# Streamed projections whose left operands start at the right operands' byte offset within 512

## The chip, the cores and the metric

The kernel runs on one core of a Trainium2 chip. The metric is the device time of one execution in microseconds; lower is better. Engines are named as the profile names them: PE (matrix multiply) and PEld (its load of left operands), DVE (vector), ACT (scalar), POOL (GpSimd), SP (sync, which here only issues DMAs).

## The reference

One decoder layer on a sequence of 1024 tokens, model width 1024, all in float32:

```python
h = rmsnorm(x, g_mix)
z = h @ w_in                                   # 1024 x 7168
rnn_x, rnn_y, conv_b, conv_c, conv_x, gate_rnn, gate_conv = split(z)
rnn_x = causal_depthwise_conv(rnn_x, conv4_w) + conv4_b
y_rnn = gelu(rnn_y) * rg_lru(rnn_x, ...)       # gates: block diagonal products, then a scan over tokens
y_conv = conv_b * causal_depthwise_conv(conv_c * conv_x, conv3_w)
merged = sigmoid(gate_rnn) * y_rnn + sigmoid(gate_conv) * y_conv
x = x + merged @ w_out
g, u = split(rmsnorm(x, g_ffn) @ w_gate_up)    # 1024 x 5632
x = x + (silu(g) * u) @ w_down
x = x + sigmoid(rmsnorm(x, g_ple) @ w_ple_gate) * (p @ w_ple)
return rmsnorm(x, g_final)
```

## The kernel before

Every float32 product is done in three passes over exact halves of its operands: `split` rounds an operand to a high half (ACT, a copy into float32r) and subtracts it for the low half (DVE), and `mm` (lines 108 to 112) issues low times high, high times low and high times high. A matmul of PE takes a left operand of 128x128, which PEld loads, and streams a right operand of 128x512 past it. The big products use Strassen's scheme in Winograd's form: seven block products in place of eight.

There are five stages. The head computes `p @ w_ple` and the first norm. The **input projection** (line 728) and **gate/up** (line 797) are the two streamed projections: `stream` (line 207) keeps the seven right operands, made of the activations, in tiles of the pool `ops`, and streams the weights through as left operands. For each product it loads a quarter of 128x512 (`part`), adds quarters where the scheme wants it, and makes the left operand `wop` of it, in `high` (line 248, ACT) and `low` (line 253, DVE). A product is 12 matmuls. The input projection has 28 pairs of channel blocks, so 28 x 7 x 12 = 2352 matmuls, and the recurrence that runs between them adds 192 (`rg`); gate/up has 22 pairs, 1848 matmuls. Between and behind these stages the **output projection** and **down** (`outer`, line 336) make both operands in `ops`, and the per-layer gate (line 860) ends the program.

A scheduler sets the order on each engine from the order of the code and from priorities; `stream` makes an operand two products ahead of its use. The only DMAs that POOL issues are some loads of the output projection and of down (`load` with `nc.gpsimd`, lines 746, 819 and 822); all others are SP's.

Where a tile lies follows from the pools. At the bottom of each partition of SBUF lie 16,384 bytes of scratch for the DMA descriptors that POOL makes, then constants, then `ops` (seven tiles of 16,384 bytes), the small tiles `sm`, and above them the pools of the stage: `w1`, `w2`, `ws`, `wp`, `ev`, `e0`, `wq` (line 205). The left operands lie in `wp` and `wq`; the last two of every seven products use `wq`. Before the change the starts are these, as remainders modulo 512 bytes (all the pieces of an operand that a matmul reads lie a multiple of 512 bytes from its start):

| operand | pool | remainder |
|---|---|---|
| right operands of both streamed projections; both operands of `outer` | `ops` | 128 |
| left operands `wop`, both streamed projections | `wp` | 320 |
| both operands of the recurrence's products, `xo` and `rg_w` | `wp` | 320 |
| left operands `wop`, input projection | `wq` | 448 |
| left operands `wop`, gate/up | `wq` | 320 |

`wq` differs between the stages since the four tiles of `e0` below it are 516 floats in the input projection (2064 bytes, padded to 2080) and 512 floats in gate/up.

## Time and profile before

| | us |
|---|---|
| median of three runs | 1460.82 |
| the three runs | 1458.82 to 1462.44 |
| span of the profiled execution, first to last instruction | 1458.2 |
| its own time outside the span | not listed; the runs lie 0.6 to 4.2 above the span |
| PE busy | 1437.6 (99%) |
| DVE, ACT busy | 1077.8 (74%), 781.7 (54%) |
| input projection on PE | 44.4 to 633.8 |
| output projection and norm on PE | 633.8 to 716.1 |
| gate/up on PE | 716.1 to 1143.8 |
| down, gate, last norm | 1143.8 to 1458.2 |

The busy time of a matmul in the profile includes its run through the array, which overlaps with the next matmul's (393 ns each, though they start some 230 ns apart). So the pace of PE is read from start to start: in the timeline, where consecutive matmuls with the same operands' names are merged to one row, the start of a row less the start of the row before, divided by the count.

### The profile page before, as it was taken

What the parts mean: (1) busy time and instruction counts of PE and PEld (TensorE: products, weight loads), DVE (VectorE), ACT (ScalarE), POOL (GpSimd) and SP (SyncE); (2) the same over time, 40 slices, a digit from 0 to 9 for tenths busy, and PEclk for the clock granted to TensorE, in tenths of its full rate; (3) what the DMA queues carried; (4) which work ended last, traced back from release to release, by engine and by line L of the source; (5) the groups of instructions that cost most, each with busy time, mean ns of one, the idle gap of its engine ahead of it and who ended that gap; (6) DMA issues with size and microseconds to landing.
All of it is one profiled execution on the core that took longest, in us unless ns stands there. A gap on an engine that the chain in (4) does not pass through costs nothing.

```text
span 1458.2 us, 17521 instructions
## 1 busy us (share of the span) xinstructions
PE 1437.6 (99%) x6348; PEld 1176.0 (81%) x6348; DVE 1077.8 (74%) x1617; ACT 781.7 (54%) x1214; POOL 10.6 (1%) x20
## 2 busy tenths in 40 slices
PE   8999999999999999999999999999999999999997
PEld 6787888888888888878888888888888888888886
DVE  6989757965697669689796555555554899995854
ACT  7757746754775467545773333333333343346764
POOL 0000000000000000000000000000000000000000
PEclk9999999999999999999999999999999999999999
DMA  8321221122112211381522222222223761524431
GB/s 317 111 87 51 75 77 52 52 79 74 53 55 75 77 51 59 111 286 53 172 81 101 87 82 85 87 88 83 76 80 106 255 231 37 195 87 141 148 145 58
DMA packets 76742, 153.77 MB, mean 105 GB/s; under 512 B 7920, under 2 KB 7920, under 8 KB 76656
## 3 DMA queue, kind: packets, MB, share of 16 engines
q1 hardware_dynamic: 74768, 145.84, 29.9%
q0 software_dynamic: 1888, 6.82, 1.4%
q8 instruction: 50, 0.82, 0.2%
q14 instruction: 36, 0.29, 0.1%
HBM read 120.12 MB, written 32.51 MB: 105 GB/s over the span
## 4 chain that ended last, share of the span: by engine, by line
PE 90%; DVE 3%; DMA 3%; ACT 2%; issue 1%; SPq 0%; DVEq 0%; ACTq 0%
PE X L111 46%; PE Y L111 23%; PE Z L111 11%; PE pg L874 6%; PE rg L111 3%; PE tp L151 1%; DMA pe_d<-peo 1%; DMA xt<-x_d 1%; DMA xt<-in_x 0%; ACT b L85 0%; DVE a11b L100 0%; DMA act_d<-a 0%; DMA a<-m_d 0%; DMA m_d<-v 0%; DVE v L722 0%
## 5 line engine op out<-in xcount | busy, mean ns | idle before, releaser
L111 PE MATMUL X<-t,wop 128*128 128x512 f32 x1800 | 431.3, 393 | 0.0
L111 PEld LDWEIGHTS X<-t,wop 128*128 128x128 f32 x1800 | 338.2, 188 | 76.6 <-DVE wop L254 0.3
L250 ACT CAST wop<-part 128x512 fp32r<-128x512 f32 x300 | 183.7, 621 | 213.8 <-PE X L111 67.4
L254 DVE TENSOR_TENSOR wop<-part,wop 128x512 fp32r<-128x512 f32 x300 | 204.8, 689 | 89.0 <-ACT wop L250 87.8
L111 PE MATMUL Z<-b,wop 128*128 128x512 f32 x600 | 146.7, 393 | 0.4 <-ACT r_late L192 0.4
L111 PE MATMUL X<-b,wop 128*128 128x512 f32 x600 | 147.0, 393 | 0.0
L111 PE MATMUL Y<-b,wop 128*128 128x512 f32 x600 | 146.4, 393 | 0.0
L111 PE MATMUL Y<-t,wop 128*128 128x512 f32 x600 | 146.2, 393 | 0.0
L111 PEld LDWEIGHTS Z<-b,wop 128*128 128x128 f32 x600 | 112.5, 188 | 26.8 <-ACT r_late L192 0.9
L111 PEld LDWEIGHTS Y<-b,wop 128*128 128x128 f32 x600 | 112.8, 188 | 25.5
L111 PEld LDWEIGHTS Y<-t,wop 128*128 128x128 f32 x600 | 112.8, 188 | 25.2
L111 PEld LDWEIGHTS X<-b,wop 128*128 128x128 f32 x600 | 112.6, 188 | 24.6
L874 PE MATMUL pg<-b,a 128*128 128x512 f32 (+1 forms) x408 | 88.4, 378 | 0.0
L111 PE MATMUL X<-t,s 128*128 128x512 f32 x360 | 85.8, 392 | 0.0
L874 PEld LDWEIGHTS pg<-b,a 128*128 128x128 f32 x408 | 73.4, 188 | 14.6
L254 DVE TENSOR_TENSOR wop<-s,wop 128x512 fp32r<-128x512 f32 x50 | 34.5, 689 | 59.5 <-ACT wop L250 59.5
L111 PEld LDWEIGHTS X<-t,s 128*128 128x128 f32 x360 | 66.8, 188 | 13.9 <-DVE t L86 0.5
L271 ACT COPY p<-Y 128x512 f32<-128x512 f32 x50 | 29.2, 583 | 72.6 <-PE Y L111 72.6
L271 ACT COPY s<-X 128x512 f32<-128x512 f32 x50 | 29.2, 588 | 59.2 <-PE X L111 58.9
L271 ACT COPY u<-X 128x512 f32<-128x512 f32 x50 | 29.2, 584 | 49.6 <-PE X L111 49.1
L435 DVE TENSOR_TENSOR xt<-X,xt 128x512 f32<-128x512 f32 x64 | 43.8, 686 | 14.5 <-PE X L111 13.6
L111 PE MATMUL rg<-xo,rg_w 128*128 128x512 f32 x192 | 47.1, 393 | 0.1
(172 smaller groups left out, 1939.7 us busy)
## 6 DMA issues: line engine op xcount, KB each, us to landing
part<-in_w_in SPq DMA_DIRECT2D x120, 256.0 KB, 2.6
part<-in_w_gu SPq DMA_DIRECT2D x96, 256.0 KB, 2.7
act_d<-a SPq DMA_DIRECT2D x44, 256.0 KB, 2.4
x_d<-xt SPq DMA_DIRECT2D x32, 256.0 KB, 2.0
bc<-in_w_down SPq DMA_DIRECT2D x10, 512.0 KB, 5.8
a<-act_d SPq DMA_DIRECT2D x10, 512.0 KB, 5.9
xt<-in_x SPq DMA_DIRECT2D x8, 512.0 KB, 8.0
pe_d<-peo SPq DMA_DIRECT2D x16, 256.0 KB, 2.9
```

What stands on the lines that cost most here:

```text
L111: nc.tensor.matmul(ps, lhs(i), rhs(j), start=start and first and n == 0, stop=last and n == 2, skip_group_check=not start)
L151: nc.tensor.transpose(ps[:, b * P:(b + 1) * P], xt[b][:, kk * P:(kk + 1) * P], ident)
L250: nc.scalar.copy(t[:, 0], s)
L254: sub(t[:, 1], s, t[:, 0].bitcast(F32))
L271: nc.scalar.copy(t, ps)
L435: add(piece, ps, piece)
L874: nc.tensor.matmul(ps, left[k // 4](i, k % 4)[:, c:c + P], right[k // 4, dh][:, j, k % 4, r], start=n + k == 0, stop=n == 2 and k == 7)
```

## The change

Three edits of sizes; no instruction is added or taken away, and on every engine the instructions stand in the same order with the same waits. The DMA scratch is halved to 8,192 bytes, which moves all tiles down by 8,192 and makes room. A filler of 320 bytes, `line`, lies between `sm` and the pools of the stages. The tiles that the input projection takes from `e0` get 544 floats (2,176 bytes, four are 8,704 = 17 x 512), of which 516 are used. With that `ops`, `wp`, `wq` of both stages, and `w1`, `w2`, `ws` and `ev` all start at remainder 128. The rest of the difference takes comments and docstrings out.

```diff
     sm = ctx.enter_context(tc.tile_pool(name="sm", bufs=2))
+
+    ctx.enter_context(tc.tile_pool(name="line", bufs=1)).tile([P, 80], F32, name="line")
     pp = ctx.enter_context(tc.tile_pool(name="pp", bufs=8, space=bass.MemoryType.PSUM))
...
         def ztile(name, early=False):
-            return (sp["e0"] if early else zp).tile([P, H + 4], F32, tag="z", name=name)
+
+            return (sp["e0"].tile([P, 544], F32, tag="z", name=name)[:, 0:H + 4] if early
+                    else zp.tile([P, H + 4], F32, tag="z", name=name))
...
-    nc = bacc.Bacc("TRN2", target_bir_lowering=False, num_devices=1)
+    nc = bacc.Bacc("TRN2", target_bir_lowering=False, num_devices=1, dynamic_dma_scratch_size=8192)
```

| operand | before | after |
|---|---|---|
| `ops` | 128 | 128 |
| `wp` (`wop`, `xo`, `rg_w`) | 320 | 128 |
| `wq`, input projection | 448 | 128 |
| `wq`, gate/up | 320 | 128 |

## Rows read from the trace of the kernel before

**Rows 1.** Page, part 1: busy us (share of the span) and instructions.

```profile
span 1458.2 us, 17521 instructions
PE 1437.6 (99%) x6348; PEld 1176.0 (81%) x6348; DVE 1077.8 (74%) x1617; ACT 781.7 (54%) x1214; POOL 10.6 (1%) x20
```

**Rows 2.** Stretches: length, busy us (instructions) of each engine, PE clock, DMA.

```profile
44.40:633.80 589.40, 589.25 (x2547) 478.15 (x2546) 453.04 (x724) 366.54 (x565) 1.56 (x2) 1.00 0.23 74
716.10:1143.80 427.70, 427.23 (x1881) 350.10 (x1880) 265.58 (x385) 172.37 (x288) 2.54 (x4) 1.00 0.28 91
```

**Rows 3.** Timeline, PE, input projection: start, us, engine, line, operands, count.

```profile
314.36 2.95 PE L111 MATMUL X<-t,wop 128*128 128x512 f32 x12
317.15 2.96 PE L111 MATMUL Z<-b,wop 128*128 128x512 f32 x12
319.95 2.92 PE L111 MATMUL Y<-b,wop 128*128 128x512 f32 x12
322.71 5.66 PE L111 MATMUL X<-t,wop 128*128 128x512 f32 x24
328.20 2.91 PE L111 MATMUL Y<-t,wop 128*128 128x512 f32 x12
...
333.70 2.96 PE L111 MATMUL X<-t,wop 128*128 128x512 f32 x12
336.50 2.96 PE L111 MATMUL Z<-b,wop 128*128 128x512 f32 x12
339.30 2.96 PE L111 MATMUL Y<-b,wop 128*128 128x512 f32 x12
342.10 5.76 PE L111 MATMUL X<-t,wop 128*128 128x512 f32 x24
347.70 2.96 PE L111 MATMUL Y<-t,wop 128*128 128x512 f32 x12
```

**Rows 4.** Timeline, PE, gate/up.

```profile
819.70 5.66 PE L111 MATMUL X<-t,wop 128*128 128x512 f32 x24
825.20 2.91 PE L111 MATMUL Y<-t,wop 128*128 128x512 f32 x12
```

**Rows 5.** Timeline, PE, output projection and down: both operands in `ops`.

```profile
658.02 11.04 PE L111 MATMUL Y<-t,s 128*128 128x512 f32 x48
668.90 11.09 PE L111 MATMUL X<-t,s 128*128 128x512 f32 x48
679.83 11.04 PE L111 MATMUL Y<-b,s 128*128 128x512 f32 x48
...
1151.97 8.32 PE L111 MATMUL Z<-b,a 128*128 128x512 f32 x36
1160.13 8.32 PE L111 MATMUL Y<-t,s 128*128 128x512 f32 x36
```

**Rows 6.** Timeline, PE, two products of the recurrence between products of the stream.

```profile
231.02 2.89 PE L111 MATMUL rg<-xo,rg_w 128*128 128x512 f32 x12
233.75 2.93 PE L111 MATMUL Y<-b,wop 128*128 128x512 f32 x12
236.51 2.93 PE L111 MATMUL rg<-xo,rg_w 128*128 128x512 f32 x12
239.28 2.93 PE L111 MATMUL X<-t,wop 128*128 128x512 f32 x12
```

**Rows 7.** Chain that ended last, around 102 to 135: start, us, what.

```profile
102.80 0.59 ACT z L512
...
134.63 0.71 DVE xo L578
135.38 2.59 PE rg L111 x10
```

**Rows 8.** The same chain at the ends of the two streamed stages.

```profile
622.86 2.76 PE Y L111 x12
...
1132.98 2.76 PE Y L111 x12
```

**Rows 9.** POOL's timeline: its DMA issues, and what it waited for.

```profile
625.92 1.56 POOL L392 DMA_DIRECT2D b<-in_w_out  x2 [624.61 <-DMA bc<-in_w_out]
1138.78 1.28 POOL L392 DMA_DIRECT2D b<-in_w_down  x2 [511.31 <-DVE b L86]
```

**Rows 10.** DMA view: POOL's issues, KB each, median us from issue to landing.

```profile
b<-in_w_down POOLq DMA_DIRECT2D x5, 512.0 KB, 5.1
a<-act_d POOLq DMA_DIRECT2D x5, 512.0 KB, 6.2
```

## The prediction

> **What bounds the kernel now.** The page's first part comes first: PE is busy 99% of the span, DVE 74%, ACT 54% [rows 1]. That alone doesn't say that PE is limited by its own pace, since a busy matmul may be a slow one. [...]

> Then the timeline, read from start to start. Where both operands lie in `ops`, at the same remainder of 128, 48 matmuls take 668.90 - 658.02 = 10.88 us, and 36 take 1160.13 - 1151.97 = 8.16 us [rows 5]: **226.7 ns** each, in two stages and with very different neighbours. In gate/up, with the left operand at 320, 24 matmuls take 825.20 - 819.70 = 5.50 us, **229** ns each [rows 4]. In the input projection the products that use `wq` (remainder 448) take 317.15 - 314.36 = 2.79 and 336.50 - 333.70 = 2.80 us for 12, **233** ns each; those behind them that use `wp` (320) run now at 5.49 / 24 = 229 ns (322.71 to 328.20), now at 5.60 / 24 = 233 ns (342.10 to 347.70) [rows 3]. All of these are matmuls of the same shape at the same clock with no wait between them. The pace differs by where the left operand lies, and `wp` products in the input projection take over the pace of one of two patterns, depending on what ran before them. The same `wp` products in gate/up, where no product lies at 448, stay at 229.

> The recurrence's products are the near miss that tells most. Both of their operands lie at 320: the same remainder, but not 128. One of them takes 233.75 - 231.02 = 2.73 us for 12 [rows 6], 227.5 ns: near the pace of `outer`, with the excess over 226.7 only 0.1 us per product, though it comes from a product at another remainder and is followed by one. So what counts is the difference of the two starts, not that the left one is at 128.

> **The change part by part.** *Offsets.* Order, waits, sizes and data are as before; so the work on PE is the same matmuls at another pace. Price per matmul after: 226.7 ns by the rows of `outer` [rows 5] at the best, 227.5 by the recurrence's row [rows 6] at the worst of the rows with equal remainders that I take as the nearest; I use 226.8, since the rows of `outer` have both operands at 128, which is what all will have. The slower pieces that the rows of `outer` also hold (679.83 - 668.90 = 10.93 us for 48, 227.7 ns) are one in several.

> Input projection: 589.25 us over 28 x 7 x 12 + 192 = 2544 matmuls is 231.6 ns, and without the few tenths of a us by which busy time overlaps a wait or runs past the last start about 231.4. Times (231.4 - 226.8) = 4.6 ns, that is **11.7 us**. Gate/up: 1848 matmuls, 228.9 ns from the steady row (5.50 / 24 = 229.2, and rounding of 0.01 us on 24 is worth 0.4 ns), less 226.8, is 2.1 ns each: **3.9 us**. The gate at the end has 96 matmuls whose left operand lies at 320 in a pool that moves along; at gate/up's 2.1 ns they are worth 0.2 us.

> *What of it lies on the path.* The chain leaves PE in three places of these stages. From 102.80 to 135.38 it runs through ACT and DVE (the first recurrence) until a `rg` product waits for `xo` [rows 7]; what PE gains in these 32.6 us only becomes a longer wait: 32.6 / 589.4 x 11.7 = 0.6 us lost. At the ends of the two stages the chain leaves PE at 622.86 + 2.76 = 625.6 and at 1132.98 + 2.76 = 1135.7 [rows 8], some 8 us before PE's last product each, for the results' way to memory and back: 8.2 / 589.4 x 11.7 = 0.2 us and 8.1 / 427.7 x 3.9 = 0.1 us lost. Everywhere else in the two stages the chain is PE.

> What would be late next: DVE. It is busy 453.04 of 589.40 us in the input projection (77%) and 265.58 of 427.70 in gate/up (62%) [rows 2], so 2% and 1% less time for the same work leave it at 79% and 63%. The one place where the chain shows it without room is the one already counted.

> *Filler and wider `e0` tiles.* No instruction reads them; the tiles' used part is the same. Cost 0. *DVE and ACT on moved tiles.* Their operands move too. No row prices that by itself; the places where they are on the path are the 32.6 us above and about 35 us at each of two stage ends, and if their instructions became 1% longer or shorter there it would be about 1 us either way. I take 0 and keep 1 us for the range. *Scratch.* POOL issues 14 DMAs in pairs, beginning with those at 625.92 and 1138.78 [rows 9], which land 5.1 to 6.2 us after their issue [rows 10]. If half the scratch never fills, the cost is 0. If it made the second DMA of a pair wait for the first to land, each pair would be 5 to 6 us later. The first pair is issued at 625.92 and PE's products that need it run behind the chain's DMAs of SP; the loads of down's later chunks are issued a product or more before their use. So I take 0; the other end is a rival below.

> Sum: 11.7 + 3.9 + 0.2 - 0.6 - 0.2 - 0.1 = **14.9 us**. The profiled span of 1458.2 becomes 1443.3. The median of the runs is 2.6 us above that span; kept above it, 1460.8 - 14.9 = **1446** us, 1.0% less.

> **The rivals.** *Where the pace comes from elsewhere.* What differs between `outer` and the stream might be what runs beside: DMA loads, copies of PSUM. Then nothing changes: 1461. Against it: the same neighbours give 229 and 233 ns in turn in the input projection [rows 3], and the recurrence's product among them 227.5 [rows 6]. [...] I give this rival 4%.

> *Disturbed at each switch.* Equal remainders might give the good pace only after some matmuls of each product, since every product of the stream takes new tiles, while those of `outer` run 36 to 48 matmuls on. If each product of 12 ran as the recurrence's does at its slower (239.28 - 236.51 = 2.77 us, 231 ns [rows 6]), the input projection would gain 2544 x 0.4 = 1 us and gate/up lose 1848 x 2 = 4 us: about 1463, no change to speak of. At half of that, 1453. Against it: those products stand between others of unequal remainders, which all lie at 128 afterwards; and `outer` changes its left operand with every matmul, and its tile in PSUM every 12. I give 5% to no gain at all and 6% to half of it.

> *Waits in PE's place.* DVE's full stretch may be longer than the chain shows, so that PE falls into waits in each of the recurrence's eight halves, not in one. If each took what PE gains in 32 us, it would be 8 x 0.6 = 5 us: 1451. It takes part in the range; the chance of it is 7%.

> *Slower: the scratch.* If the smaller scratch holds back every second DMA of POOL's seven pairs by the 5.1 to 6.2 us of a landing, and all of it reached PE, it would be 7 x 5.6 = 39 us, less the 15 gained: 1485. From four exposed pairs on the kernel is slower by more than 0.3%. Against it: the pairs are issued one or more products ahead, a product being 8.2 to 10.9 us [rows 5], and a stage's second load is not used before its first. 3%.

> **How the numbers follow.** The forecast of 1446 has 75%, the waits 7% (1451), half the gain 6% (1453), no gain 9% in two forms (1461 to 1463), slower 3% (1485). About 0.3% (4.4 us) is what a measurement of this kernel can tell from no change. Faster by more, that is below 1456.4: 75 + 7 + 6 = 88%; within it 9%; slower 3%. The forecast's own spread: 226.4 to 227.5 ns per matmul is -1.8 to +3.1 us on 4392 matmuls, 1 us for DVE and ACT, and the runs differ by 2 us from their median. Low end 1446 - 4.5, about 1441.5; the high end takes in the waits and half the gain, 1453. What lies outside is 12% and the tails of the forecast.

> **What would show it.** Right: in the changed kernel's timeline every 12 matmuls of either stream take 2.72 us and 24 take 5.44, with no difference between `wq` and `wp` products; the input projection is some 11 us shorter, gate/up some 3.8; `outer` keeps 10.88 for 48; the wait for `xo` near 135 us grows by about half a microsecond; POOL's issues and landings stay. Wrong, if 229 or 233 ns stays anywhere in the streams (the offset isn't the cause, or isn't all of it), if `rg` or `wop` waits of PE appear in every head, or if DMAs of POOL land later than 6.2 us.

## The result, and the profile after

The changed kernel takes **1446.4 us** (median of four runs, 1443.95 to 1446.51) against 1461.0 for the kernel before beside it: a ratio of **0.989** (95% interval 0.987 to 0.991), 14.6 us less. The forecast was 1446, in a range of 1441.5 to 1453.

First the page of the changed kernel, part 1 (busy us, share of the span, instructions), and of part 5 (busy us, mean ns of one) the largest group of loads of left operands, before and after:

```profile
span 1444.7 us, 17521 instructions
PE 1421.6 (98%) x6348; PEld 1174.9 (81%) x6348; DVE 1076.7 (75%) x1617; ACT 780.5 (54%) x1214; POOL 10.6 (1%) x20
...
L111 PEld LDWEIGHTS X<-t,wop 128*128 128x128 f32 x1800 | 338.2, 188 | 76.6 <-DVE wop L254 0.3
...
L113 PEld LDWEIGHTS X<-t,wop 128*128 128x128 f32 x1800 | 337.8, 188 | 70.8 <-DVE wop L256 0.8
```

The instructions are the same in number [rows 1]. PE's busy time fell by 16.0 us, DVE's and ACT's by about 1 us each. The load of a left operand takes 188 ns as before: the slow pace can't be seen in its duration, only in the starts of the matmuls.

The stretches from the first to the last matmul of the two streams (length, busy us of PE, PEld, DVE, ACT and POOL, granted clock, DMA share and GB/s):

```profile
43.60:621.60 578.00, 577.50 (x2546) 477.50 (x2545) 453.07 (x726) 365.79 (x566) 1.56 (x2) 1.00 0.24 75
706.60:1130.50 423.90, 423.26 (x1882) 349.93 (x1882) 265.66 (x385) 172.46 (x289) 2.54 (x4) 1.00 0.28 92
```

Against [rows 2], and with the bounds of the stages between them:

| us in the profiled execution | before | after | difference |
|---|---|---|---|
| head, until the first matmul of the input projection | 44.4 | 43.6 | -0.8 |
| input projection | 589.4 | 578.0 | -11.4 |
| output projection and norm | 82.3 | 85.0 | +2.7 |
| gate/up | 427.7 | 423.9 | -3.8 |
| down, gate, last norm | 314.4 | 314.2 | -0.2 |
| span | 1458.2 | 1444.7 | -13.5 |

The timeline of PE in the changed kernel (start, us, operands, count): first the recurrence between products of the input projection, as in [rows 6], then gate/up as in [rows 4], then the output projection as in [rows 5].

```profile
227.22 2.88 PE L113 MATMUL rg<-xo,rg_w 128*128 128x512 f32 x12
229.94 2.88 PE L113 MATMUL Y<-b,wop 128*128 128x512 f32 x12
232.66 2.88 PE L113 MATMUL rg<-xo,rg_w 128*128 128x512 f32 x12
235.38 6.74 PE L113 MATMUL X<-t,wop 128*128 128x512 f32 x29
...
809.52 5.60 PE L113 MATMUL X<-t,wop 128*128 128x512 f32 x24
814.96 2.88 PE L113 MATMUL Y<-t,wop 128*128 128x512 f32 x12
...
648.59 11.04 PE L113 MATMUL Y<-t,s 128*128 128x512 f32 x48
659.47 11.09 PE L113 MATMUL X<-t,s 128*128 128x512 f32 x48
```

From start to start a product of 12 takes 2.72 us, a pair of 24 takes 814.96 - 809.52 = 5.44, and 48 in the output projection take 10.88: 226.7 ns each, in all of them. The recurrence's products too run at 2.72, where one took 2.73 and the next 2.77 before. One pace is left in these rows.

### The profile page after: what moved, and what is told of

It reads as the page before. It is cut to its first block, busy times and chain, and to the rows that moved or that the text cites. A ratio compares the mean times of both kernels' runs of the same rounds, so it can differ in the third digit from the quotient of the medians.

```text
span 1444.7 us, 17521 instructions
## 1 busy us (share of the span) xinstructions
PE 1421.6 (98%) x6348; PEld 1174.9 (81%) x6348; DVE 1076.7 (75%) x1617; ACT 780.5 (54%) x1214; POOL 10.6 (1%) x20
## 4 chain that ended last, share of the span: by engine, by line
PE 92%; DVE 3%; ACT 2%; DMA 1%; issue 1%; SPq 0%; ACTq 0%; DVEq 0%
PE X L113 46%; PE Y L113 23%; PE Z L113 11%; PE pg L878 6%; PE rg L113 3%; PE ple L113 1%; PE tp L153 1%; DVE xt L437 1%; ACT r L171 1%; DMA xt<-in_x 0%; DMA wple<-in_w_ple 0%; DVE wop L256 0%; ACT wop L252 0%; DVE b L88 0%; DVE v L726 0%
## 5 line engine op out<-in xcount | busy, mean ns | idle before, releaser
L113 PE MATMUL X<-t,wop 128*128 128x512 f32 x1800 | 424.5, 389 | 0.3 <-DVE wop L256 0.3
```

The costliest lines, as they stand in the source:

```text
L113: nc.tensor.matmul(ps, lhs(i), rhs(j), start=start and first and n == 0, stop=last and n == 2, skip_group_check=not start)
```

## Experiments

The paces below are read as above, from start to start in PE's timeline, in rows of 24 matmuls where there are such. The difference is that of the left operand's start from the right one's, as a remainder.

### The scratch alone

Theory: the pace depends on the difference of the operands' starts. Rival: the gain is the scratch's, or that of where the tiles lie absolutely.

```diff
-    nc = bacc.Bacc("TRN2", target_bir_lowering=False, num_devices=1)
+    nc = bacc.Bacc("TRN2", target_bir_lowering=False, num_devices=1, dynamic_dma_scratch_size=8192)
```

> The kernel before with the DMA scratch halved and nothing else: all tiles move down by 8192 bytes, the remainders within 512 stay (wp 320, wq 448 and 320). Offset theory: nothing changes, 1461 us, input projection 589 us on PE (231.4 ns per matmul), gate/up 428 us (229 ns). Theory that the gain came from the scratch or from the absolute place of the tiles: 1446 us. Theory that the smaller scratch holds POOL's DMAs back: above 1465 us, with landings of more than 6.2 us.

Measured: 1460.5 us, a ratio of 1.0003 (0.9992 to 1.0014). The stretches of its two streams, in the columns of before:

```profile
43.60:632.60 589.00, 588.85 (x2546) 478.05 (x2545) 453.74 (x726) 367.05 (x566) 1.56 (x2) 1.00 0.23 74
715.30:1143.00 427.70, 427.24 (x1881) 350.09 (x1880) 265.70 (x385) 172.36 (x288) 2.54 (x4) 1.00 0.28 91
```

They are those of [rows 2]. POOL's loads land 4.7 to 6.2 us after their issue, like those of [rows 10]. All tiles moved by 8,192 bytes and half the scratch is gone, and nothing happened: the scratch neither gives nor costs.

### The wide early tiles without the filler

```diff
-    ctx.enter_context(tc.tile_pool(name="line", bufs=1)).tile([P, 80], F32, name="line")
```

(against the changed kernel). Every left operand then lies 192 past the right one.

> The change without the filler: scratch halved and the wide early tiles. Left operands lie at 320 in both pools of both stages, 192 past the right ones. Offset theory, with the 233 ns of wp products in the input projection taken over from wq products at 448: with no product at 448 left, every product runs at 229 ns as in gate/up; the input projection shrinks from 589 to 583 us, gate/up stays at 428, in all about 1455 us. Theory that the 233 ns of wp products belongs to their neighbours in that stage (DMAs, copies) and not to 448: the input projection stays near 589 and the whole at 1460.

Measured: 1455.7 us, 0.9965 (0.9954 to 0.9976). PE's timeline in its input projection:

```profile
301.51 5.66 PE L112 MATMUL X<-t,wop 128*128 128x512 f32 x24
307.01 2.91 PE L112 MATMUL Y<-t,wop 128*128 128x512 f32 x12
309.75 2.91 PE L112 MATMUL X<-b,wop 128*128 128x512 f32 x12
312.50 2.91 PE L112 MATMUL X<-t,wop 128*128 128x512 f32 x12
315.25 2.91 PE L112 MATMUL Z<-b,wop 128*128 128x512 f32 x12
317.99 2.91 PE L112 MATMUL Y<-b,wop 128*128 128x512 f32 x12
```

All at 229 ns; no product at 233 as in [rows 3]. `wp` did not move against `ops` here, only `wq` did, and yet `wp` products that ran at 233 ns before run at 229 now. So their 233 ns were taken over from products with `wq` at 448, and not the work of their neighbours in the stage. The input projection takes 584.4 us, 5.0 less than before. That it is not the 583 expected has two reasons in the trace, at least: its first matmuls run at a lower granted clock (0.76 from 40 to 47 us), and the recurrence's products, which the expectation had put at 229 ns too, keep 230 between products at another remainder.

### The filler without the wide early tiles

```diff
-            return (sp["e0"].tile([P, 544], F32, tag="z", name=name)[:, 0:H + 4] if early
-                    else zp.tile([P, H + 4], F32, tag="z", name=name))
+            return (sp["e0"] if early else zp).tile([P, H + 4], F32, tag="z", name=name)
```

> The change without the wide early tiles: scratch halved and the filler. Difference 0 for wp in both stages and for wq in gate/up; 128 for wq in the input projection. Offset theory: gate/up 424 us at 226.7 ns; the input projection's wp products at 226.7 ns unless a wq product leaves them a slower pace; the wq products at a pace of their own for a difference of 128, that no row shows yet (226 to 236 ns). In all 1446 to 1452 us. Theory that the wide tiles matter by themselves (the DVE or ACT work on them): their absence shows as longer DVE instructions on z tiles.

Measured: 1448.9 us, 0.9923 (0.9902 to 0.9945). PE's timeline in its input projection; the rows at 310.54 and 313.33 are products with `wq` (difference 128), the others with `wp` (difference 0):

```profile
307.82 2.89 PE L113 MATMUL X<-b,wop 128*128 128x512 f32 x12
310.54 2.95 PE L113 MATMUL X<-t,wop 128*128 128x512 f32 x12
313.33 2.96 PE L113 MATMUL Z<-b,wop 128*128 128x512 f32 x12
316.13 2.89 PE L113 MATMUL Y<-b,wop 128*128 128x512 f32 x12
318.87 5.60 PE L113 MATMUL X<-t,wop 128*128 128x512 f32 x24
324.31 1.07 PE L113 MATMUL Y<-t,wop 128*128 128x512 f32 x4
```

Within one stage, with the same neighbours, the products at 128 take 2.79 and 2.80 us and those around them 2.72 to 2.74. After a slow product the pace of a difference of 0 is back at once (318.87 to 324.31 is 5.44). The filler alone gives most of the gain; the wide tiles are worth what is left, 648 matmuls by 6 ns, 4 us of the input projection (582.5 against 578.0). That the wide tiles would matter by the work of DVE on them is not borne out: its instructions on `z` tiles take the same time in both kernels (a median of 747 ns without them and 746 with them for the 48 of line 570, line 571 in the changed kernel), and in the input projection it is busy 453.69 us without the wide tiles and 453.07 with them.

### Equal starts at another remainder

```diff
+    ctx.enter_context(tc.tile_pool(name="low", bufs=1)).tile([P, 48], F32, name="low")
     ops = ctx.enter_context(tc.tile_pool(name="ops", bufs=7))
```

> The change with 192 more bytes of filler ahead of ops: all operands, left and right, lie at 320 instead of 128, all differences 0. Theory that the difference counts: 226.7 ns everywhere, 1446 us. Theory that an operand must lie at 128 (or at a multiple of 128) itself: at 320 the streamed projections run at 229 ns or more and the output projection and down, which ran at 226.7, slow down too: 5976 matmuls by 2.3 ns or more, 1460 us or above.

Measured: 1445.3 us, 0.9894 (0.9876 to 0.9911). PE's timeline, input projection and gate/up:

```profile
316.92 5.60 PE L114 MATMUL X<-t,wop 128*128 128x512 f32 x24
322.36 2.88 PE L114 MATMUL Y<-t,wop 128*128 128x512 f32 x12
...
806.67 5.60 PE L114 MATMUL X<-t,wop 128*128 128x512 f32 x24
812.11 2.88 PE L114 MATMUL Y<-t,wop 128*128 128x512 f32 x12
```

5.44 us for 24 in both. At 320 the left operands were slow while the right ones lay at 128; with both at 320 they are not. The difference counts, not the place.

### The pace at other differences

Four kernels, each the change with a pad ahead of the stage's pools, of one size in the input projection and another in gate/up; and two in which the left operands are cut out of wider tiles, 16, 96, 160 or 240 bytes past their start. Those tiles lie 4,352 bytes (17 x 256) apart, so that in these two kernels each stage holds two differences, 256 bytes from each other. Each of the six ran once.

```diff
     with ExitStack() as st:
+        pool(st, "pad", 1).tile([P, 16], F32, name="pad")
         sp = stream_pools(st)
```

```diff
-            t = pools[...].tile([P, 2, 4, P], F32R, tag="wop", name="wop")
+            o = (240 if n_pairs == NF else 16) // 4
+            t = pools[...].tile([P, 1088], F32R, tag="wop", name="wop")
+            t = t[:, o:o + 1024].rearrange("p (s k c) -> p s k c", s=2, k=4)
```

> The change with a pad ahead of the stages' pools: left operands start 64 bytes past the right ones (within 512) in the input projection and 256 past in gate/up; the recurrence's products keep a difference of 0. The pad also reorders some instructions, so the pace of the products is what counts. Offset theory: each stage has a pace of its own that differs from 226.7 ns, between 226 and 236; rg products near 227 to 231 since they follow others. Theory that only the remainder within 64 or 256 matters: 226.7 ns for one or both.

> As the one before with differences of 128 (input projection) and 384 (gate/up). Offset theory: paces of their own, 226 to 236 ns. In the kernel with the filler alone, wq products at a difference of 128 ran among wp products at 0; here all run at 128, so that the pace is not mixed.

> Differences of 448 (input projection) and 320 (gate/up). 320 is that of the wq products of the kernel before: 233 ns expected in all of gate/up, so 1848 x 6.5 = 12 us more there than at 0, 436 us. 448 has no row: 226 to 236 ns.

> Differences of 32 (input projection) and 480 (gate/up), the smallest steps that a tile can be moved by. Offset theory: if the cost grows with the distance from 0, both lie near 227; if any difference costs the same, both lie at 229 to 233.

> The change with left operands cut out of tiles of 4352 bytes (17 x 256), 16 bytes past an equal remainder within 256 in the input projection and 240 past in gate/up. The wider tiles reorder some instructions, so only the pace counts. If the pace gets worse gradually with the distance, both lie between 226.7 and 229 ns; if any difference costs the full price, 233 (or 229 for 240, as for 192). A pace under 226.7 would show that 0 isn't the best difference; no theory here expects that.

> As the one before with differences of 96 (input projection) and 160 (gate/up) within 256. Between 64, 128 (233 ns each) and 192 (229 ns) the theory of the difference within 256 expects 233 for 96 and 229 to 233 for 160.

The moved pools also change the order of instructions, and a stage's first work starts later (in the kernel with 128 and 384 PE waits 3.9 us for DVE and 2.1 us more before gate/up); that the reason is tiles which now overlap more than one tile of the stage before is likely, and not shown. Their times, 1465 to 1487 us, are no measure of the pace and aren't used. PE's timeline of the kernel with 64 (input projection) and 256 (gate/up):

```profile
306.18 5.76 PE L113 MATMUL X<-t,wop 128*128 128x512 f32 x24
311.78 2.96 PE L113 MATMUL Y<-t,wop 128*128 128x512 f32 x12
...
819.48 5.60 PE L113 MATMUL X<-t,wop 128*128 128x512 f32 x24
824.92 2.88 PE L113 MATMUL Y<-t,wop 128*128 128x512 f32 x12
```

At 64 bytes 24 matmuls take 5.60 us, at 256 they take 5.44, the pace of a difference of 0. So the expectation of a pace of its own for 256 fell, and that of its rival, a remainder within 256, came true. And of the kernel with 448 and 320:

```profile
301.00 5.66 PE L113 MATMUL X<-t,wop 128*128 128x512 f32 x24
306.49 2.91 PE L113 MATMUL Y<-t,wop 128*128 128x512 f32 x12
...
810.63 5.76 PE L113 MATMUL X<-t,wop 128*128 128x512 f32 x24
816.23 2.96 PE L113 MATMUL Y<-t,wop 128*128 128x512 f32 x12
```

448 gives 5.49, like 192 [rows 4]; 320 gives 5.60, like 64. The kernel with 16 bytes in the input projection shows two paces, one after the other:

```profile
96.16 2.96 PE L113 MATMUL Y<-t,wop 128*128 128x512 f32 x12
98.96 2.92 PE L113 MATMUL rg<-xo,rg_w 128*128 128x512 f32 x12
101.72 2.88 PE L113 MATMUL X<-t,wop 128*128 128x512 f32 x12
104.44 2.88 PE L113 MATMUL rg<-xo,rg_w 128*128 128x512 f32 x12
```

Up to the row at 96.16 its products take 2.80 us for 12, 233 ns each. Behind the first products of the recurrence, whose difference is 0 or 256, they take 2.72, and 2.72 is what they take in the rows from 300 to 330 us too. All differences, read in the same way, between 299 and 326 us or 805 and 830:

| difference in bytes | remainder within 256 | us for 24 | ns each |
|---|---|---|---|
| 0, 256 | 0 | 5.44 | 226.7 |
| 16, 272 | 16 | 5.44; 5.60 ahead of the recurrence | 226.7; 233 |
| 32 | 32 | 5.60 | 233 |
| 64, 320 | 64 | 5.60 | 233 |
| 96, 352 | 96 | 5.62 | 234 |
| 128, 384 | 128 | 5.60 | 233 |
| 160, 416 | 160 | 5.60 | 233 |
| 192, 448 | 192 | 5.49 | 229 |
| 480 | 224 | 5.60 | 233 |
| 240, 496 | 240 | 5.48 | 228 |

Four pairs 256 bytes apart, in kernels or stages of their own, have the same pace, so it is the remainder within **256** that counts, not within 512. The pace doesn't rise evenly with the distance: 32 bytes cost the full 6.6 ns, and 192 and 240 lie between that and nothing. The rows of 16 and 240 taken alone would fit a gradual rise (226.7 and 228 ns), but the others don't, and 16 bytes cost the full 6.6 ns as well until the recurrence's first products had run. The full price expected for 240, 229 ns, was missed narrowly. No difference ran below 226.7 ns. And the pace is not one number per difference: products at 16 ran at 227 or 233 ns, and in the kernel before, products at 192 ran at 229 or 233 ns [rows 3]. Of the others one pace each was seen; those of 32, 64, 96 and 128 came back to 233 or 234 ns behind the recurrence's products.

### The smallest change that makes the differences multiples of 256

```diff
     sm = ctx.enter_context(tc.tile_pool(name="sm", bufs=2))
+    ctx.enter_context(tc.tile_pool(name="line", bufs=1)).tile([P, 16], F32, name="line")
...
-            return (sp["e0"] if early else zp).tile([P, H + 4], F32, tag="z", name=name)
+            return (sp["e0"].tile([P, 528], F32, tag="z", name=name)[:, 0:H + 4] if early
+                    else zp.tile([P, H + 4], F32, tag="z", name=name))
```

(against the kernel before, with the scratch of 16,384 bytes.)

> The kernel before with its full DMA scratch of 16384 bytes, a filler of 64 bytes and early tiles of 528 floats, 192 bytes more per partition in all, which just fit: left operands lie at 384 in wp and, in gate/up, in wq (256 past the right ones), and at 128 in wq in the input projection (difference 0). Theory that the remainder of the difference within 256 counts: 226.7 ns in both streams, 1446 us, as the change. Theory that it is the remainder within 512: wp products keep a slow pace (229 to 233 ns), 1455 to 1470 us, with fast wq products in the input projection alone.

Measured: 1444.6 us, 0.9893 (0.9876 to 0.9909). Input projection (`wp`, difference 256) and gate/up:

```profile
316.61 5.60 PE L112 MATMUL X<-t,wop 128*128 128x512 f32 x24
322.05 2.88 PE L112 MATMUL Y<-t,wop 128*128 128x512 f32 x12
...
809.09 5.60 PE L112 MATMUL X<-t,wop 128*128 128x512 f32 x24
814.53 2.88 PE L112 MATMUL Y<-t,wop 128*128 128x512 f32 x12
```

5.44 us in both. So the whole gain is to be had with 192 bytes per partition, no smaller scratch, and differences that are not 0 within 512. Its ratio and the change's (0.9891) can't be told apart.

### The output projection, 2.7 us longer

The one stage that went the wrong way. PE's timeline of the changed kernel around its wait, with the reason in brackets, and the stretch of 9 us around it (length; busy us of the engines; granted clock; DMA):

```profile
641.38 7.37 PE L113 MATMUL Z<-b,a 128*128 128x512 f32 x24 [3.28 <-DVE a L88]
...
637.00:646.00 9.00, 5.72 (x18) 4.23 (x18) 6.26 (x8) 2.71 (x4) 0.00 (x0) 0.81 0.80 293
```

PE waits 3.28 us for the operand `a`, and the granted clock of the stretch is 0.81, against 1.00 in the 9 us around the same wait of the kernel before (649 to 658): the matmuls from 643.0 to 645.5 us, behind the wait, run at a granted clock of 0.50. From 641.38 to 648.59 the 24 take 7.21 us, and at 226.7 ns they would take 5.44, so by this estimate the clock costs about 1.8 us, and the wait, 2.1 us in the kernel before, about 1.2 more. DVE's timeline shows what is ahead of `a`:

```profile
638.72 1.47 DVE L437 TENSOR_TENSOR xt<-X,xt 128x512 f32<-128x512 f32 x2 [0.93 <-DMA xt<-in_x]
```

DVE waits 0.93 us for a load of x ahead of the step that PE waits for, the low half of `a` at 640.11. To see whether these loads set the wait, the four of them that come first were given to POOL's queue:

```diff
-            nc.sync.dma_start(out=xt[b]..., in_=src[...])
+            eng = nc.gpsimd if src is x and b < 4 and dh == 0 else nc.sync
+            eng.dma_start(out=xt[b]..., in_=src[...])
```

> The change, with the four x loads that the output projection's first results wait for (token blocks 0 to 3, first half of the columns) issued by POOL, not by SP behind its last loads of m_d. In the changed kernel SP issues them from 632.31 on, DVE waits 0.93 us for one, and PE waits 3.3 us for DVE before product 2, after which the granted clock of the stretch is 0.81. Theory that the longer output projection (85.0 us against 82.3 before) comes from those loads: they are issued 1 to 2 us earlier, PE's wait falls to 2.2 us or less, the clock stays at 1.00, and the output projection takes 82 to 83 us; in all 1444 us. Theory that it is DVE's order and the loads of m_d: PE's wait stays at about 3 us and the time at 1446. In both the streams keep 226.7 ns.

Measured: 1449.7 us, 0.9917 (0.9894 to 0.994): some 3 us more than the change in the medians, though the two ratios' intervals overlap. In the profiled executions the streams are as long as in the change (578.0 and 423.7 us), and the output projection takes 89.7 us. Three of the loads were issued at 632.10, 0.2 us ahead of SP's at 632.31, and landed later. PE's timeline, then one line each of the chain that ended last, from the kernel before, the changed one and this one (start, us, what):

```profile
644.13 6.23 PE L113 MATMUL Z<-b,a 128*128 128x512 f32 x18 [6.21 <-DVE a L88]
...
642.66 4.78 DMA a<-m_d
...
632.31 6.38 DMA xt<-in_x
...
633.17 8.99 DMA xt<-in_x
```

The remedy failed: by the trace POOL could not issue the three before an earlier load of x had landed, at 631.9, and they took 9.0 us, not 6.4. Neither expectation came true. Nor does the run tell its two theories apart, since the edit changed DVE's order too: here all four additions of x stand ahead of `a`, in the changed kernel two. What the chains show is which load came last ahead of `a`: in the kernel before the reading back of `m_d`, in the changed kernel and in this one a load of x; it landed 3.5 us later here, and PE's wait grew from 3.3 to 6.2.

Whether the change itself lengthened the wait is another matter, and the other runs speak against it: by the same view it is 2.1 us in the kernel before, 2.4 with the scratch alone, 2.9 with the wide tiles, 1.9 with the filler alone, 2.2 with equal starts at 320, 2.8 with the small change, and 3.3 in the change. The kernel with equal starts at 320 has the change's pace throughout and an output projection of 82.3 us. So the 2.7 us likely belong to how the loads fell in that execution: there is one profiled execution of each, and of the changed kernel's four runs one is more than 2.3 us shorter than the other three.

## Why the prediction was right

**What bounds the kernel.** Right: PE's pace, start to start. The gain of the two streams is the pace alone; in them no wait was taken away, and there was nearly none to take [rows 2].

**The price per matmul.** Forecast 226.8 ns, measured 226.7 in both streams. Input projection 11.7 us less the 0.6 that DVE takes, 11.1, against 11.4; gate/up 3.9 against 3.8; the gate's 0.2 against 0.2 for all that stands behind gate/up, too little to be told from no change. The step that carried this was to take the price from a stage of the same kernel that had equal remainders already [rows 5].

**That the difference counts, not the place.** Argued from the recurrence's row [rows 6]; shown by the equal starts at 320 and by the differences of 256. What the prediction left as it stood was the 512 of the change's title: the period is 256. It made no difference to the sum, as a multiple of 512 is one of 256.

**That `wp` products take over a pace.** Shown by the wide tiles without the filler: with no product at 320 left, none at 192 ran at 233 ns. What the prediction left open is open still: behind products at 320 they ran now at 229 and now at 233 [rows 3], and no run tells what decides it.

**The first recurrence.** Forecast: PE's wait near 135 us grows by half a microsecond, at `xo`. By the view of waits it grew by that much, but at the step before, `wop`; the wait for `xo` stayed at 0.6. From the kernel before and from the changed one (us in total, times, longest):

```profile
PEld X L111 <- DVE wop L254: 0.3, 1, 0.3
PEld rg L111 <- DVE xo L578: 0.6, 1, 0.6
```

```profile
PEld X L113 <- DVE wop L256: 0.8, 1, 0.8
PEld rg L113 <- DVE xo L582: 0.6, 1, 0.6
```

The stretch of ACT and DVE was the bound and stayed it: in the chain it is 32.6 us long before (102.80 to 135.38) and 32.5 after (101.06 to 133.55).

**The output projection.** This is the term that was mis-sized: 0.2 us lost there in the sum, 2.7 us longer in the profile. The sum took the way through memory at the stage's end as fixed. It has a spread of its own, of about 1.4 us in the wait over seven kernels, and in two of them, the change and the small change, a lower granted clock (0.81 from 637 to 646 us in both) adds to it. The head, 0.8 us shorter, fell the other way, and there it is the clock: from 39 to 46 us the granted clock was 0.76 in the kernel before and 1.00 in the changed one. The profiled spans differ by 13.5 us. In the medians the sum is close, 14.6 us against 14.9, and that close by luck: these two terms, and the runs of one kernel (2.6 us apart for the changed one, 3.6 for the one before), are all larger than the 0.3 us that are left.

**The rivals.** The pace doesn't come from elsewhere: the filler alone has both paces side by side in one stage. The offset of the left operand costs 6.6 to 7.5 ns on 226.7 per matmul at differences of 32 to 160 bytes. There is no disturbance at each switch of product once all differences are 0: the rows at 227.22 to 235.38 have none. In the streams waits did not come in PE's place, but for the half microsecond above. The scratch alone changed nothing that its interval (0.1% either way) would show.

## What to carry to other kernels

Where PE is busy without waits, read its matmuls from start to start and compare stages of the same shape: a few per cent between them can be a fault in the layout, as here (229 and 233 ns against 226.7), and a stage that has the better pace gives the price. Lay the left operands so that they start a multiple of 256 bytes from the right ones that are streamed past them (226.7 ns a matmul in both streams of the three kernels laid so: the change, the equal starts at 320 and the small change; shown for float32r operands of this one shape); a filler of 64 bytes and tile sizes that keep it so were enough here, for 1.1%. Check it per stage, since a tile that is padded in one stage only moves every pool above it.

## What the runs showed of the hardware that was not expected

After PE's wait of 3.3 us in the output projection the granted clock of the stretch was 0.81. By the same view it was 0.66 (640 to 650 us) in the kernel in which the wait was 6.2, 0.81 in the small change, where it was 2.8, and 1.00 with the wide tiles, where it was 2.9, and with equal starts at 320, where it was 2.2. So waits of nearly the same length came with either clock.
